# A hybrid encoder layer on one core: the convolution's layer norm goes from the first stage to the last, taps cover 1,024 tokens, and the projections get a fourth PSUM buffer

## The chip, the cores and the metric

The kernel runs on one core of one Trainium2 chip, as one launch. The metric is the device time of one execution, in microseconds (us); lower is better. An execution takes a little longer than the span of the profile, which goes from the first to the last instruction. Engines are named as in the profile: PE (TensorE matmuls), PEld (its weight loads), DVE (VectorE), ACT (ScalarE), POOL (GpSimd) and SP (SyncE, which here issues nearly all DMAs, in order, from one queue).

## What is computed

One encoder layer with the same weights for two groups of tokens, 2,048 and 1,024 of them, all float32. From `h = x @ w_in + b_in` (1,024 features in, 5,632 out, split in nine) two branches follow: a depthwise convolution of 31 taps with a layer norm and gates, and a differential attention with four heads. They are merged by sigmoid gates, projected, added to the input and normalised. The lines that matter here:

```python
u = glu_a * jax.nn.sigmoid(glu_b)
u = conv(u, conv_dw) + conv_dw_b            # 31 taps along the tokens, 512 channels
u = silu(layer_norm(u, conv_ln_g, conv_ln_b)) * silu(conv_gate)
y_conv = u @ w_conv_proj + b_conv_proj
...
merged = sigmoid(m_conv) * y_conv + sigmoid(m_attn) * (o @ w_attn_o)
out = layer_norm(ALPHA * x + merged @ w_out + b_out, ln_g, ln_b)
```

The layer norm of the convolution needs, for each token, the mean and the variance over all 512 channels. The channels lie on partitions, 128 to a tile, so these sums go over four channel tiles and over the partitions; the sum over partitions is a matmul with a matrix of constants (`ones_c`).

## The kernel before

**Precision.** Each float32 operand of a matmul is split into a rounded high part and the remainder (`split`, `split_w`: ACT copies, then DVE or POOL subtracts), and each product is three matmuls: high by high, low by high, high by low (`mm3`, `mm`).

**Phase A (0 to about 1549 us): the input projection.** Three blocks of 1,024 tokens, (group 0, first half), (group 0, second half), (group 1). In each, 22 weight pieces of 256 output features are worked through in the order of L211: GLU_B, GLU_A, GLU_B+1, GLU_A+1, K, CGATE, K+1, CGATE+1, Q, AGATE, and so on, then V and the merge gates. A piece has two output tiles, each 128 features by 1,024 tokens: 48 matmuls of 512 columns into one PSUM tile `psA` (L291). I count tiles from 0, so that tiles 2, 3, 6 and 7 are GLU_A, tiles 8 and 9 are K, 10 and 11 are CGATE, and so on. There are three `psA` buffers (L108), and two small ones, `psB`, for the layer norm. A tile is evacuated by `evac`: GLU_A by DVE (L238), K and Q by ACT and DVE (L254, L255; then the rotation by POOL at L259 and L260, and DVE at L262), gates by ACT and DVE (L242, L243), the merge gates by ACT alone (L248). POOL also makes the low part of every weight piece (`wl`, L127, two per piece).

The convolution runs in the same phase on DVE. GLU_A's product is written to DRAM (`ud`, L239); a generator, `conv_chunk`, handles 512 tokens of all four channel tiles. It loads `uc` (L150), does 31 taps for each channel tile (L156 the first, L159 the others; two channel tiles in turn), sums the tiles on POOL (L164 to L166), gets the mean by two matmuls (`total`, L139), subtracts it (L173), squares (L177), gets the variance in the same way, takes root and reciprocal (L186, L189), applies scale, gain, bias and SiLU (L193 to L198), and stores the result `sd` (L199). `pump` advances this generator by 6 or 11 steps after each output tile. The order of instructions on the engines in this phase and in phase C is set by a scheduler at build time; each engine then runs its list in order.

**Phase B (about 1549 to 2230 us): attention,** with an order written out by hand on PE, DVE, ACT and POOL: scores (L505), softmax, the combination of the two maps on POOL (L525 to L527, each with `e` of 128x1024), turns through the PE (L534, `tp`, copied out by ACT L536 and DVE L541), products (L95 to L97 into `ops`), and the sums of squares for the sub-layer norm (L566, L90 `sql`). At the end of it `prepare` (L419) makes the first input of phase C: it loads `sd` and the convolution's gate `cgd`, multiplies (L428) and splits the product into `uh` and `ul`.

**Phase C (about 2230 us to the end): merge and output.** Six rows of 512 tokens. For each row `merge` has eight steps of 24 matmuls (12 with `uh`, `ul` and 12 with `oh`, `ol`, into `y`, L95 to L97) and `project` has two halves of 96 matmuls (into `z`). The inputs of the next row are prepared during the projection of this one: `u` in its first half, `o` in its second. DVE also finishes each row (L705 to L722), and POOL makes the low part of each piece of `w_out` (`zl`).

Of the kernel before, what the change touches and what calls it, by code (L numbers as in the profile page):

```python
# [43 lines left out]
def encoder_kernel(ctx: ExitStack, tc: tile.TileContext, t: dict):  # L44
# [54 lines left out]
    # ---------------------------------------------------------------- phase A  # L99
    with ExitStack() as st:  # L100
# [34 lines left out]
        def total(x):  # L135
            """The mean over the channels, on every partition, of what the partitions hold of it."""
            ps = psB.tile([P, 512], F32, name="psB")
            for i, part in enumerate(split(cv, "tt", x, [P, 512], 1, nc.gpsimd)):
                nc.tensor.matmul(ps, ones_c, part, start=i == 0, stop=i == 1)  # L139
            return ps  # L140

        def conv_chunk(g, n):
            """The depthwise convolution of 512 tokens, its layer norm and SiLU, a step at a time."""
            t0 = n * 512
            acc = cv.tile([P, CT, 512], F32, name="acc")
            for c0 in range(0, CT, 2):
                us = []
                for c in (c0, c0 + 1):
                    u = cv.tile([P, 512 + 2 * HALO], F32, name="uc", bufs=3)
                    nc.sync.dma_start(u, ud[g][c][:, t0:t0 + 512 + 2 * HALO])  # L150
                    us.append(u)
                for k in range(TAPS):
                    for c in (c0, c0 + 1):
                        src = us[c - c0][:, k:k + 512]
                        if k == 0:
                            nc.vector.tensor_scalar(acc[:, c], src, dw_sb[:, c, 0:1], cvec[:, 0, c:c + 1],  # L156
                                                    op0=ALU.mult, op1=ALU.add)
                        else:
                            nc.vector.scalar_tensor_tensor(acc[:, c], src, dw_sb[:, c, k:k + 1], acc[:, c],  # L159
                                                           op0=ALU.mult, op1=ALU.add)  # L160
                        yield
            tmp = lambda: cv.tile([P, 512], F32, name="cvtmp", bufs=4)
            sm, sm2 = tmp(), tmp()
            nc.gpsimd.tensor_add(sm, acc[:, 0], acc[:, 1])  # L164
            nc.gpsimd.tensor_add(sm2, acc[:, 2], acc[:, 3])
            nc.gpsimd.tensor_add(sm, sm, sm2)  # L166
            for _ in range(4):
                yield
            mean = total(sm)
            for _ in range(3):  # L170
                yield
            for c in range(CT):
                nc.vector.tensor_sub(acc[:, c], acc[:, c], mean)  # L173
                yield
            for c in range(CT):
                s = cv.tile([P, 512], F32, name="cvsq", bufs=2)
                nc.scalar.activation(s, acc[:, c], AF.Square)  # L177
                if c:
                    nc.gpsimd.tensor_add(s, q2, s)
                q2 = s  # L180
                yield
            for _ in range(4):
                yield
            var = total(q2)
            sd_, rs = tmp(), tmp()
            nc.scalar.activation(sd_, var, AF.Sqrt, bias=eps_t)  # L186
            for _ in range(3):
                yield
            nc.vector.reciprocal(rs, sd_)  # L189
            for _ in range(5):  # L190
                yield
# [644 lines left out]
```

## Time and profile before

| | |
|---|---|
| time, median of 3 runs | 2825.17 us (2818.87 to 2825.88) |
| span of the profiled execution | 2816.1 us |
| PE busy | 2709.3 us (96%), 13,818 matmuls |
| DVE, ACT, POOL busy | 1843.1, 1074.4, 1478.5 us |
| phase A, 0 to 1549 us | PE 1478.49, DVE 862.90, POOL 653.03 us busy |
| 1549 to 2230 us (attention) | PE 671.07, DVE 595.87, POOL 603.76 us busy |
| 2300 to 2816 us (most of phase C) | PE 495.84, DVE 339.88, POOL 192.32 us busy |

The median of the runs lies 9.1 us above the span of the profiled execution, whose own time is close to that: what lies around the span is start and end of the execution. How to read the rows further down: a row of a timeline gives the start in us, the duration of the group in us, the engine, the line of the kernel, the operation, what it writes and reads by the program's names, the size, and in square brackets how long the engine sat idle before it and what it then waited for. A group's duration goes to the recorded end of its last instruction; the start of the next row on the same engine shows how long it really took from the queue. A row of the waits gives engine, tile and line, what ended the wait, the total in us, how often, and the longest.

### The profile page before, as it was taken

How to read it: one execution, taken by the hardware profiler on the slowest of the kernel's cores; microseconds unless marked ns; L12 is line 12 of the kernel's file. 1: busy time of each engine (PE TensorE's matmuls, PEld its weight loads, DVE VectorE, ACT ScalarE, POOL GpSimd, SP SyncE). 2: the span in 40 equal slices, each digit the busy share in tenths (PEclk: the TensorE clock that was granted, in tenths of full speed). 3: DMA queues.
4: the chain of work that ended last, by engine and by line, in shares of the span. 5: the costliest groups of instructions: out<-in, count | busy, mean ns of one | idle time of the engine just before them, and what ended most of it. 6: DMA issues, size and time to landing. Idle time of an engine off the chain costs nothing. (4 is left out here: it accounts for less than half of the span.)

```text
span 2816.1 us, 36981 instructions
## 1 busy us (share of the span) xinstructions
PE 2709.3 (96%) x13818; PEld 2274.5 (81%) x13818; DVE 1843.1 (65%) x2564; ACT 1074.4 (38%) x1540; POOL 1478.5 (53%) x774
## 2 busy tenths in 40 slices
PE   9989999998999998979999999999999999999998
PEld 7868988887897877858878788888888877777777
DVE  4961110396387495994940888888888866667665
ACT  3122132212322222213121788878788822222121
POOL 3554232245535424546442899988888833333343
PEclk9999999999999999989999999999999999999999
DMA  6245323324443343334333332322234375566553
GB/s 194 71 152 179 126 105 112 143 72 158 157 142 119 108 138 104 105 127 156 105 116 112 109 85 88 85 69 70 69 94 116 104 253 190 182 207 200 181 162 119
DMA packets 194980, 364.89 MB, mean 130 GB/s; under 512 B 25088, under 2 KB 98288, under 8 KB 194800
## 3 DMA queue, kind: packets, MB, share of 16 engines
q1 hardware_dynamic: 193792, 362.22, 40.1%
q8 instruction: 109, 1.79, 0.3%
q14 instruction: 71, 0.58, 0.1%
q10 hardware_dynamic: 1008, 0.29, 0.1%
HBM read 242.67 MB, written 107.18 MB: 124 GB/s over the span
## 5 line engine op out<-in xcount | busy, mean ns | idle before, releaser
L127 POOL TENSOR_TENSOR wl<-raw,wh 128x1024 fp32r<-128x1024 f32 (+1 forms) x138 | 416.5, 3038 | 485.6 <-ACT wh L126 471.8
L291 PE MATMUL psA<-xh,wh 128*128 128x512 f32 x1920 | 600.6, 395 | 37.7 <-DVE ev L255 16.5
L159 DVE SCALAR_TENSOR_TENSOR acc<-uc,conv_dw,acc 128x512 f32<-128x512 f32 x720 | 608.5, 896 | 5.8
L291 PE MATMUL psA<-xl,wh 128*128 128x512 f32 x1920 | 598.6, 393 | 0.9 <-DVE xl L284 0.9
L291 PE MATMUL psA<-xh,wl 128*128 128x512 f32 x1920 | 597.7, 393 | 0.3 <-POOL wl L127 0.3
L291 PEld LDWEIGHTS psA<-xh,wh 128*128 128x128 f32 x1920 | 365.4, 191 | 116.9 <-DVE ev L255 17.8
L291 PEld LDWEIGHTS psA<-xl,wh 128*128 128x128 f32 x1920 | 365.4, 190 | 78.8 <-DVE xl L284 1.6
L291 PEld LDWEIGHTS psA<-xh,wl 128*128 128x128 f32 x1920 | 364.6, 190 | 77.6 <-POOL wl L127 1.0
L527 POOL TENSOR_TENSOR e<-e 128x2048 f32<-128x2048 f32 (+1 forms) x96 | 373.1, 3887 | 8.0
L505 PE MATMUL s<-km,qq 128*128 128x512 f32 x1280 | 352.3, 397 | 4.8 <-DVE e L507 4.4
L518 ACT ACTIVATE e<-e,mx 128x2048 f32<-128x2048 f32 (+1 forms) x192 | 329.5, 1716 | 1.2 <-DVE e L507 1.1
L507 DVE TENSOR_SCALAR_CACHE_REDUCE e<-s 128x1024 f32<-128x1024 f32 x192 | 233.4, 1216 | 77.1 <-PE s L505 75.7
L541 DVE TENSOR_TENSOR al<-tp,ah 128x512 fp32r<-128x512 f32 x320 | 220.1, 688 | 56.1 <-ACT ah L536 56.1
L505 PEld LDWEIGHTS s<-km,qq 128*128 128x128 f32 x1280 | 219.7, 189 | 41.3 <-DVE e L507 10.7
L126 ACT ACTIVATE wh<-raw 128x1024 fp32r<-128x1024 f32 (+1 forms) x138 | 134.0, 1012 | 285.0 <-PE psA L291 164.9
L536 ACT ACTIVATE ah<-tp 128x512 fp32r<-128x512 f32 x320 | 189.5, 593 | 98.7 <-PE tp L534 96.1
L90 POOL TENSOR_TENSOR zl<-zraw,zh 128x512 fp32r<-128x512 f32 x88 | 123.8, 1409 | 162.4 <-ACT zh L89 142.5
L95 PE MATMUL ops<-ah,vv 128*128 128x256 f32 x640 | 207.3, 324 | 0.2 <-ACT row L567 0.2
L534 PEld LDWEIGHTS tp<-ident,e 128*128 128x128 f32 x1280 | 158.6, 141 | 48.6 <-DVE al L541 3.7
L534 PE MATMUL tp<-ident,e 128*128 128x128 f32 x1280 | 193.3, 274 | 4.5 <-POOL e L527 3.0
L97 PE MATMUL ops<-al,vv 128*128 128x256 f32 x640 | 180.7, 282 | 0.7 <-DVE al L541 0.7
L96 PE MATMUL ops<-ah,vv 128*128 128x256 f32 x640 | 179.7, 281 | 0.0
(165 smaller groups left out, 4259.5 us busy)
## 6 DMA issues: line engine op xcount, KB each, us to landing
raw<-in_w_in SPq DMA_DIRECT2D x130, 512.0 KB
qq<-qd SPq DMA_DIRECT2D x384, 64.0 KB
zraw<-in_w_out SPq DMA_DIRECT2D x88, 256.0 KB
ev<-ev SPq DMA_DIRECT2D x96, 128.0 KB
kd<-ev SPq DMA_DIRECT2D x24, 512.0 KB
qd<-ev SPq DMA_DIRECT2D x24, 512.0 KB
vd<-ev SPq DMA_DIRECT2D x24, 512.0 KB
mcd<-evm SPq DMA_DIRECT2D x24, 512.0 KB
```

Source lines behind the costliest of these rows:

```text
L95: nc.tensor.matmul(ps, ah, bh, start=first, stop=False)
L97: nc.tensor.matmul(ps, ah, bl, start=False, stop=last)
L127: nc.gpsimd.tensor_sub(lo, raw, hi.bitcast(F32))
L159: nc.vector.scalar_tensor_tensor(acc[:, c], src, dw_sb[:, c, k:k + 1], acc[:, c], op0=ALU.mult, op1=ALU.add)
L291: nc.tensor.matmul(ps[:, n * 512:(n + 1) * 512], w[a][:, k, j * P:(j + 1) * P], B.xs[k][x][:, n * 512:(n + 1) * 512], start=k == 0 and a = ...
L505: nc.tensor.matmul(s[:, n * 512:(n + 1) * 512], p.qt[2 * c + i][:, j * P:(j + 1) * P], p.km[c, hf][:, n * 512:(n + 1) * 512], start=i == 0 ...
L507: nc.vector.tensor_scalar(p.e[j, c][:, hf * 1024:(hf + 1) * 1024], s, -SCALE, mx[:, hf - 1:hf] if hf else None, op0=ALU.mult, op1=ALU.min, ...
L518: nc.scalar.activation(e, e, AF.Exp, bias=p.mx[j, c][:, nh - 1:nh], scale=-1.0, accum_out=sc)
L527: nc.gpsimd.tensor_add(e0, e0, e)
L534: nc.tensor.transpose(tp[:, i, j * P:(j + 1) * P], p.e[j, 0][:, kt * P:(kt + 1) * P], ident)
L536: nc.scalar.activation(ah, tp, AF.Copy)
L541: nc.vector.tensor_sub(al, tp, ah.bitcast(F32))
```

## The change

**The convolution.** `conv_chunk` becomes `conv_unit`: one channel tile and about 1,024 tokens (1,008, 1,040 and 1,024 in the three blocks, so that each block's taps need only what is there). A unit has one load of `uc`, 31 taps of that width (after: L144, L146) and one store of the plain convolution to `sd` (L148). Four units per block, 372 taps in all where there were 744 of 512 tokens. `uc` and `acc` have two buffers each. `pump` advances by 4 steps after each tile in every block.

**The layer norm** and SiLU leave phase A and stand in `prepare_u`, a generator with eight steps: load four tiles of `sd`; sum them on POOL (`sum4`, L403 to L405, the split at L407 and L408); two matmuls for the mean (L414); subtract and square (L424, L426), sum again; two matmuls for the variance; root and reciprocal (L432, L433) and the loads of `cgd`; and twice two tiles of scale (L443), sigmoid (L444), gain and bias (L445), gate times sigmoid on POOL (L446), product (L447) and split. For the first row these steps stand at the end of phase B, with PSUM taken from the turns' buffers `tp`; for the other five they stand in the projection of the row before, with PSUM taken from `y`. The `o` branch is unchanged, under the name `prepare_o`.

**PSUM.** With `psB` gone, `psA` has four buffers in place of three.

Comments are dropped, and one build setting (`dynamic_dma_scratch_size=1024`) is added.

```diff
-        psA = pool(name="a_ps", bufs=3, space=PSUM)
-        psB = pool(name="a_ps2", bufs=2, space=PSUM)
+        psA = pool(name="a_ps", bufs=4, space=PSUM)
...
-            rate = 6 if bi == 0 else 11
+            rate = 4
...
-                todo = [0, 1] if B.g else ([0] if B.b == 0 else [1, 2, 3])
-                convs += [conv_chunk(B.g, n) for n in todo]
+                t0, t1 = {(0, 0): (0, TB - 16), (0, 1): (TB - 16, 2 * TB), (1, 0): (0, TB)}[B.g, B.b]
+                convs += [conv_unit(B.g, i, t0, t1) for i in range(CT)]
...
+        def conv_unit(g, c, t0, t1):
+            n = t1 - t0
+            u = cv.tile([P, CONV_N + 2 * HALO], F32, name="uc", bufs=2)[:, :n + 2 * HALO]
+            nc.sync.dma_start(u, ud[g][c][:, t0:t1 + 2 * HALO])
+            acc = cv.tile([P, CONV_N], F32, name="acc", bufs=2)[:, :n]
+            for k in range(TAPS):
+                src = u[:, k:k + n]
+                if k == 0:
+                    nc.vector.tensor_scalar(acc, src, dw_sb[:, c, 0:1], cvec[:, 0, c:c + 1], op0=ALU.mult, op1=ALU.add)
+                else:
+                    nc.vector.scalar_tensor_tensor(acc, src, dw_sb[:, c, k:k + 1], acc, op0=ALU.mult, op1=ALU.add)
                 yield
+            nc.sync.dma_start(sd[g][c][:, t0:t1], acc)
...
+    def prepare_u(R, ps):
+        g, r = R.g, slice(R.t0, R.t0 + 512)
+        xs = []
+        for i in range(CT):
+            xs.append(cin.tile([P, 512], F32, name="lx", bufs=CT))
+            nc.sync.dma_start(xs[i], sd[g][i][:, r])
+        tmp = lambda tag: cin.tile([P, 512], F32, name="l" + tag, tag=tag, bufs=2)
+        def sum4(parts):
+            a, b = tmp("x1"), tmp("x2")
+            nc.gpsimd.tensor_add(a, parts[0], parts[1])
+            nc.gpsimd.tensor_add(b, parts[2], parts[3])
+            nc.gpsimd.tensor_add(a, a, b)
+            hi, lo = (cin.tile([P, 512], F32R, name="lm" + x, tag="rb", bufs=2) for x in "hl")
+            nc.scalar.activation(hi, a, AF.Copy)
+            nc.gpsimd.tensor_sub(lo, a, hi.bitcast(F32))
+            return hi, lo
+        def mean(parts):
+            m = ps()
+            for i, part in enumerate(parts):
+                nc.tensor.matmul(m, ones_c, part, start=i == 0, stop=i == 1)
+            return m
+        yield
+        parts = sum4(xs)
+        yield
+        m = mean(parts)
+        yield
+        sq = []
+        for x in xs:
+            nc.vector.tensor_sub(x, x, m)
+            sq.append(cin.tile([P, 512], F32, name="lq", bufs=CT))
+            nc.scalar.activation(sq[-1], x, AF.Square)
+        parts = sum4(sq)
+        yield
+        m = mean(parts)
+        yield
+        rs = tmp("x1")
+        nc.scalar.activation(rs, m, AF.Sqrt, bias=eps_t)
+        nc.vector.reciprocal(rs, rs)
+        gates = []
+        for i in range(CT):
+            gates.append(cin.tile([P, 512], F32, name="lq", bufs=CT))
+            nc.sync.dma_start(gates[i], cgd[g][i][:, r])
+        yield
+        for h in range(2):
+            for i in (2 * h, 2 * h + 1):
+                x = xs[i]
+                sg = tmp("x2")
+                nc.vector.tensor_mul(x, x, rs)
+                nc.scalar.activation(sg, x, AF.Sigmoid, bias=cvec[:, 2, i:i + 1], scale=cvec[:, 1, i:i + 1])
+                nc.vector.tensor_scalar(x, x, cvec[:, 1, i:i + 1], cvec[:, 2, i:i + 1], op0=ALU.mult, op1=ALU.add)
+                nc.gpsimd.tensor_mul(gates[i], gates[i], sg)
+                nc.vector.tensor_mul(x, x, gates[i])
+                R.ins["u"].append(split(cin, "u", x, [P, 512], 4))
+            yield
...
-                    ahead = prepare(rows[0], "u")
-                    for i in range(CT + 2):
+                    ahead = prepare(rows[0], "u", lambda: psT.tile([P, 512], F32, name="tp"))
+                    for i in range(U_STEPS):
                         late[now + 2 * i].append(lambda: next(ahead))
```

The change moves instructions at many places. Three of them are shown, each engine's own list, in order.

**DVE in the first block of phase A,** from the evacuation of tile 8 on. Before (L255 and L243 are evacuations, L159 taps, L262 the low part of the rotated K):

```order
L255 SCALAR_TENSOR_TENSOR ev<-psA,b_in_cols,cos 128x1024
L159 SCALAR_TENSOR_TENSOR acc<-uc,conv_dw,acc 128x512 x13
L262 TENSOR_TENSOR ev<-ev 128x1024
L159 SCALAR_TENSOR_TENSOR acc<-uc,conv_dw,acc 128x512 x3
L255 SCALAR_TENSOR_TENSOR ev<-psA,b_in_cols,cos 128x1024
L159 SCALAR_TENSOR_TENSOR acc<-uc,conv_dw,acc 128x512 x10
L243 SCALAR_TENSOR_TENSOR ev<-psA,b_in_cols,ev 128x1024
L159 SCALAR_TENSOR_TENSOR acc<-uc,conv_dw,acc 128x512 x2
L262 TENSOR_TENSOR ev<-ev 128x1024
L159 SCALAR_TENSOR_TENSOR acc<-uc,conv_dw,acc 128x512 x11
L243 SCALAR_TENSOR_TENSOR ev<-psA,b_in_cols,ev 128x1024
```

Now (L203 and L191 are the evacuations, L144 and L146 taps, L210 the low part):

```order
L203 SCALAR_TENSOR_TENSOR ev<-psA,b_in_cols,cos 128x1024
L146 SCALAR_TENSOR_TENSOR acc<-uc,conv_dw,acc 128x1008 x7
L210 TENSOR_TENSOR ev<-ev 128x1024
L146 SCALAR_TENSOR_TENSOR acc<-uc,conv_dw,acc 128x1008
L203 SCALAR_TENSOR_TENSOR ev<-psA,b_in_cols,cos 128x1024
L146 SCALAR_TENSOR_TENSOR acc<-uc,conv_dw,acc 128x1008
L144 TENSOR_SCALAR acc<-uc,conv_dw,conv_vecs 128x1008
L146 SCALAR_TENSOR_TENSOR acc<-uc,conv_dw,acc 128x1008 x5
L191 SCALAR_TENSOR_TENSOR ev<-psA,b_in_cols,ev 128x1024
```

Between two evacuations stand about as many tap elements as before, in half as many instructions. In the first block the taps of before end at tile 12; now they go on until tile 19, and 78 of them stand between the evacuation of tile 8 and that of tile 19. In the list of after the second and the third block look much the same as the first.

**POOL at the end of attention.** Before, the last two combinations of a pair (`cc`, `e`, `e`) stand behind each other:

```order
L90 TENSOR_TENSOR sql<-sq,sqh 128x256
L525 TENSOR_TENSOR cc<-cc,stats 128x1
L526 TENSOR_SCALAR e<-e,cc,neglam 128x1024
L527 TENSOR_TENSOR e<-e 128x1024
L525 TENSOR_TENSOR cc<-cc,stats 128x1
L526 TENSOR_SCALAR e<-e,cc,neglam 128x1024
```

Now the sums over the channel tiles stand between them, and those of the squares (`lq`) right behind:

```order
L91 TENSOR_TENSOR sql<-sq,sqh 128x256
L534 TENSOR_TENSOR cc<-cc,stats 128x1
L535 TENSOR_SCALAR e<-e,cc,neglam 128x1024
L536 TENSOR_TENSOR e<-e 128x1024
L403 TENSOR_TENSOR lx_18556<-lx 128x512
L404 TENSOR_TENSOR lx_18557<-lx 128x512
L405 TENSOR_TENSOR lx_18556<-lx_18556,lx_18557 128x512
L408 TENSOR_TENSOR lml<-lx_18556,lmh 128x512
L534 TENSOR_TENSOR cc<-cc,stats 128x1
L535 TENSOR_SCALAR e<-e,cc,neglam 128x1024
L536 TENSOR_TENSOR e<-e 128x1024
L91 TENSOR_TENSOR sql<-sq,sqh 128x256
```

So four instructions on POOL came in ahead of the last combination. On PE the two mean matmuls (L414) stand ahead of the last seven turns, and the two variance matmuls ahead of the last three.

**DVE at the same place.** Before, a product and a low part (L428, L90) stand between the copies of turned blocks (L541):

```order
L541 TENSOR_TENSOR al<-tp,ah 128x512 x2
L428 TENSOR_TENSOR x_19266<-x_19266,x_19267 128x512
L90 TENSOR_TENSOR ul<-x_19266,uh 128x512
L541 TENSOR_TENSOR al<-tp,ah 128x512 x2
L428 TENSOR_TENSOR x_19306<-x_19306,x_19307 128x512
L90 TENSOR_TENSOR ul<-x_19306,uh 128x512
```

Now (L424 subtracts the mean, L433 is the reciprocal, `lx_18747` the inverse root):

```order
L424 TENSOR_TENSOR lx<-lx,tp 128x512 x4
L550 TENSOR_TENSOR al<-tp,ah 128x512 x4
L433 RECIPROCAL lx_18747<-lx_18747 128x512
L550 TENSOR_TENSOR al<-tp,ah 128x512
L443 TENSOR_TENSOR lx<-lx,lx_18747 128x512
L445 TENSOR_SCALAR lx<-lx,conv_vecs 128x512
L447 TENSOR_TENSOR lx<-lx,lq 128x512
L91 TENSOR_TENSOR ul<-lx,uh 128x512
L443 TENSOR_TENSOR lx<-lx,lx_18747 128x512
L445 TENSOR_SCALAR lx<-lx,conv_vecs 128x512
L447 TENSOR_TENSOR lx<-lx,lq 128x512
```

The four channel tiles stand one behind the other: the scaling of the second tile (L443) follows the low part of the first (L91). In the rows of phase C that come later the four L443 stand together.

More of the change, by code (lines that the diff above doesn't have):

```diff
@@ L36 @@
 NE = 8
+CONV_N = TB + 16
 NST = NH * sum(LENS) // P
@@ L133, in load_w @@
             return w
[L135 to L167, printed above, removed]
-                yield
[L169 to L191, printed above, removed]
-            for c in range(CT):
-                nc.vector.tensor_mul(acc[:, c], acc[:, c], rs)
-                sg = cv.tile([P, 512], F32, name="cvsq", bufs=2)
-                nc.scalar.activation(sg, acc[:, c], AF.Sigmoid, bias=cvec[:, 2, c:c + 1], scale=cvec[:, 1, c:c + 1])
-                nc.vector.tensor_scalar(acc[:, c], acc[:, c], cvec[:, 1, c:c + 1], cvec[:, 2, c:c + 1],
-                                        op0=ALU.mult, op1=ALU.add)
-                nc.gpsimd.tensor_mul(acc[:, c], acc[:, c], sg)
-                nc.sync.dma_start(sd[g][c][:, t0:t0 + 512], acc[:, c])
-                yield
@@ L417, in __init__, with prepare, prepare_o @@
             self.ins, self.gates, self.m, self.x, self.st = {"u": [], "o": []}, [], [], [], []
-    def prepare(R, kind):
+    def prepare(R, kind, ps=None):
+        return prepare_u(R, ps) if kind == "u" else prepare_o(R)
+    def prepare_o(R):
         g, r = R.g, slice(R.t0, R.t0 + 512)
-        dst = R.ins[kind]
+        dst = R.ins["o"]
         loaded = []
@@ L425, in prepare @@
             if i >= 2:
[L426 to L432 removed]
+                x1, x2, rb = loaded.pop(0)
+                nc.vector.scalar_tensor_tensor(x1, x1, gsub, x2, op0=ALU.mult, op1=ALU.mult)
@@ L433, in prepare @@
+                nc.vector.tensor_mul(x1, x1, rb)
+                dst.append(split(mp, "o", x1, [P, 512], 4))
             if i < CT:
-                src = [d[g][i][:, r] for d in {"u": (sd, cgd), "o": (ogd, agd)}[kind]]
-                if kind == "o":
-                    src.append(rrd[g][i, r].partition_broadcast(P))
-                loaded.append([cin.tile([P, 512], F32, name=n, bufs=2) for n in ("x1", "x2", "rb")[:len(src)]])
+                src = [ogd[g][i][:, r], agd[g][i][:, r], rrd[g][i, r].partition_broadcast(P)]
@@ L438, in prepare @@
+                loaded.append([cin.tile([P, 512], F32, name=n, bufs=2) for n in ("x1", "x2", "rb")])
                 for x, y in zip(loaded[-1], src):
                     nc.sync.dma_start(x, y)
+            yield
+    U_STEPS = 8
+    def prepare_u(R, ps):
[51 more added lines that the diff above has]
+                R.ins["u"].append(split(cin, "u", x, [P, 512], 4))
@@ L775, in encoder_kernel @@
                 factors(1, io, psY.tile([P, 512], F32, name="y"))
-            steps = {kind: [lambda i=i: next(i)] * (CT + 2) if nxt else [] for kind in "uo"
-                     for i in [nxt and prepare(nxt, kind)]}
+            steps = {kind: [lambda i=i: next(i)] * n if nxt else [] for kind, n in (("u", U_STEPS), ("o", CT + 2))
+                     for i in [nxt and prepare(nxt, kind, lambda: psY.tile([P, 512], F32, name="y"))]}
             both = lambda *fs: lambda: [f() for f in fs]
```

9 lines of the change are left out of this document (1 added, 8 removed).

## The prediction

> **What bounds the kernel now.** I read the page first, then busy time by stretch, then PE's waits, then timelines where PE waits. The page and the windows:
>
> ```profile
> PE 2709.3 (96%) x13818; PEld 2274.5 (81%) x13818; DVE 1843.1 (65%) x2564; ACT 1074.4 (38%) x1540; POOL 1478.5 (53%) x774
> 0.00:1549.00 1549.00, 1478.49 (x6940) 1239.35 (x6940) 862.90 (x1011) 370.66 (x390) 653.03 (x262) 0.98 0.38 127
> 2230.00:2300.00 70.00, 63.87 (x316) 50.49 (x315) 44.41 (x56) 23.93 (x50) 29.41 (x23) 0.98 0.78 248
> 2300.00:2816.00 516.00, 495.84 (x2112) 394.78 (x2110) 339.88 (x446) 115.80 (x199) 192.32 (x133) 1.00 0.56 178
> ```
>
> The columns are the window, its length, then PE, PEld, DVE, ACT, POOL busy, the granted clock, DMA share, GB/s. PE bounds every stage: only gaps, slow clock and the edges can be won. DVE is busy 863 of 1549 us in phase A, so on average it is no limit there; the question is whether it is one in places. PE's waits:
>
> ```profile
> PE psB L139 <- ACT tth L89: 28.5, 4, 13.6
> PE psA L291 <- DVE ev L255: 16.5, 3, 6.8
> PE psA L291 <- DVE ev L243: 11.9, 4, 5.0
> PE psA L291 <- ACT xh L283: 5.4, 1, 5.4
> PE psA L291 <- ACT evm L248: 3.9, 1, 3.9
> PE psB L139 <- POOL ttl L90: 3.2, 3, 2.1
> ```
>
> Of 69 us here, 32 are the layer norm's matmuls (`psB`), which stand in PE's list ahead of projections that could run, and 32 are evacuations that come late (28 of them DVE's, behind taps). How much phase A loses in all comes from the pace of undisturbed matmuls:
>
> ```profile
> 1240.30 0.62 PE L291 MATMUL psA<-xh,wh 128*128 128x512 f32 x2
> ...
> 1256.17 0.61 PE L291 MATMUL psA<-xh,wl 128*128 128x512 f32 x2
> ```
>
> There are 35 pairs between these starts: 15.87/70 = 0.227 us a matmul, 10.88 us for a tile of 48. The 6940 of the window are 5760 such, 1152 of half the width (about 0.12) and the norm's 24: 1306 + 138 + 5 = 1449 us. So phase A loses 100 us: 69 in the waits above and the rest at a slow clock, as behind the longest wait:
>
> ```profile
> 1270.38 0.80 PE L139 MATMUL psB<-tth,ones_c 128*128 128x512 f32 x1 [13.61 <-ACT tth L89]
> ...
> 1273.85 1.05 PE L291 MATMUL psA<-xh,wh 128*128 128x512 f32 x2
> 1277.26 0.81 PE L291 MATMUL psA<-xl,wh 128*128 128x512 f32 x2
> ```
>
> The four pairs from 1273.85 to 1277.26 take 3.41 us where they take 1.81 at full pace, so a wait of this length costs about 1.6 us more. [...]
>
> **Part 1: the taps.** The first block, where K and the gates are evacuated:
>
> ```profile
> 126.34 1.28 DVE L255 SCALAR_TENSOR_TENSOR ev<-psA,b_in_cols,cos 128x1024 f32<-128x1024 f32 x1
> 127.53 16.09 DVE L159 SCALAR_TENSOR_TENSOR acc<-uc,conv_dw,acc 128x512 f32<-128x512 f32 x13
> 143.55 1.21 DVE L262 TENSOR_TENSOR ev<-ev 128x1024 f32<-128x1024 f32 x1
> 144.69 2.06 DVE L159 SCALAR_TENSOR_TENSOR acc<-uc,conv_dw,acc 128x512 f32<-128x512 f32 x3
> ...
> 147.87 6.69 DVE L159 SCALAR_TENSOR_TENSOR acc<-uc,conv_dw,acc 128x512 f32<-128x512 f32 x10
> 154.50 1.27 DVE L243 SCALAR_TENSOR_TENSOR ev<-psA,b_in_cols,ev 128x1024 f32<-128x1024 f32 x1
> ```
>
> ```profile
> 125.90 2.79 POOL L259 TENSOR_TENSOR ev<-ev,sin 128x1024 f32<-128x1024 f32 x1 [6.97 <-DMA ev<-ev]
> 128.78 2.72 POOL L260 TENSOR_TENSOR ev<-ev 128x1024 f32<-128x1024 f32 x1
> 133.62 5.48 POOL L127 TENSOR_TENSOR wl<-raw,wh 128x1024 fp32r<-128x1024 f32 x2 [2.12 <-ACT wh L126]
> ```
>
> Ten taps with POOL idle take 154.50 - 147.87 = 6.63 us, 0.663 each. Thirteen with POOL at work take 16.02: 7.4 us longer, while POOL ran 9.4 us (the last 1.2 of L259, L260 and the two L127). So 1 us of POOL costs the taps 0.79 us, and one POOL operation of 2.72 us costs DVE 2.15. The evacuation at 126.34 took 1.19 us to the next start beside POOL, so evacuations are not held up.
>
> [...]
>
> A tap of 1,024 tokens is not in the trace. Two of 512 take 1.33; the subtraction at 143.55, as wide and with two SBUF inputs, takes 1.14 to the next start. I take 1.20, nearer to the latter since one instruction's fixed part is saved. Over 372 taps that spares 372 x 0.13 = 48 us of DVE.
>
> Where DVE does not hold PE up, that is worth nothing. Where it does is counted from the order of after, with the first starts of GLU_A's evacuation and of the taps (each row: duration in ns as least, median, most; first and last start):
>
> ```profile
> L238 DVE SCALAR_TENSOR_TENSOR ev<-psA,b_in_cols,ev x12: 1271/1278/1285, 43.5 to 1112.7; 128x1024 f32<-128x1024 f32 x12
> L156 DVE TENSOR_SCALAR acc<-uc,conv_dw,conv_vecs x24: 534/547/2625, 54.5 to 1417.9; 128x512 f32<-128x512 f32 x24
> ```
>
> Tile 2 is ready at 43.5, so PE's first tile began about 10 us into the span (43.5 - 3 x 10.88), and tile 8 is ready at 10 + 9 x 10.88 = 108. In each block 46 taps stand ahead of its evacuation. From 54 us on, 46 x 1.20 + 3 x 1.19 + 7 POOL operations x 2.15 = 74, so it is evacuated at 128, much as now (126.34): DVE is 20 us behind. From there to the evacuation of tile 19 there are 78 taps, 11 evacuations of 1.19, six subtractions of 1.14 and 24 POOL operations (12 for the rotation, 12 for weights), of which one in twelve falls beside an evacuation: 93.6 + 13.1 + 6.8 + 22 x 2.15 = 161 us. PE's 11 tiles are 120. So DVE falls behind by 41 more, 61 in all. Four `psA` buffers let PE run three tiles ahead, 32.6 us (three: 21.8). The rest, 28 us, is a wait on `psA` in each block, 85 in three, and at four waits a block 1.3 us of clock each, 15. With 10 at the start, phase A would lose 110, where it now loses 100 and 5 in the norm's matmuls: **+5 us**. The gain of the removed norm (32 us of waits and 5 of matmuls) and of the fourth buffer (10.9 a block) is real, but the taps that stand spread over the second block's tiles now stand in front of tiles 8 to 19 of every block.
>
> Bounds: if a POOL operation costs DVE only 1.1 us, the wait is 28 - 23 = 5 a block, and A gains 64, some 69 with the clock; if taps cost 1.33 and POOL all of 2.72, it is 28 + 10 + 13 = 51, and A loses 75 to 80.
>
> **Part 2: the layer norm of row 0,** at the end of attention. Sizes, from the same operations in phase A of before:
>
> ```profile
> L173 DVE TENSOR_TENSOR acc<-acc,psB x24: 678/681/687, 365.0 to 1449.7; 128x512 f32<-128x512 f32 x24
> L189 DVE RECIPROCAL cvtmp<-cvtmp x6: 3352/3353/3354, 402.3 to 1474.7; 128x512 f32<-128x512 f32 x6
> L196 DVE TENSOR_SCALAR acc<-acc,conv_vecs x24: 536/598/2190, 408.1 to 1486.2; 128x512 f32<-128x512 f32 x24
> L195 ACT ACTIVATE cvsq<-acc,conv_vecs x24: 799/816/820, 406.4 to 1485.3; 128x512 f32<-128x512 f32 x24
> L195 ACT ACT_TABLE_LOAD  x6: 1283/1283/1283, 402.3 to 1474.7; - x6
> L198 POOL TENSOR_TENSOR acc<-acc,cvsq x24: 1285/1300/2297, 408.7 to 1490.4; 128x512 f32<-128x512 f32 x24
> L165 POOL TENSOR_TENSOR cvtmp<-acc x6: 1260/1265/1291, 179.7 to 1442.4; 128x512 f32<-128x512 f32 x6
> ```
>
> And where PE, ACT and POOL stand there now (from their timelines):
>
> ```profile
> 2234.13 0.60 PE L534 MATMUL tp<-ident,e 128*128 128x128 f32 x4
> 2236.56 0.63 ACT L89 ACTIVATE uh<-x 128x512 fp32r<-128x512 f32 x1 [2.04 <-DVE x L428]
> 2235.93 0.65 POOL L525 TENSOR_TENSOR cc<-cc,stats 128x1 f32<-128x1 f32 x1
> 2240.62 1.17 POOL L90 TENSOR_TENSOR sql<-sq,sqh 128x256 fp32r<-128x256 f32 x1
> 2256.96 0.54 PE L97 MATMUL y<-ul,w_conv_projh 128*128 128x512 f32 x1
> ```
>
> POOL is free for the sums at 2235.93, where the last combination stands now. Three sums, ACT's copy, the low part: 4 x 1.27 + 0.63 = 5.7, so the mean can run at 2241.6, where PE arrives at about 2234: 7.5 us of wait. The last combination (4.7) ends at 2246.4, `sql` at 2247. The subtractions (4 x 0.68, behind four copies of turns) and squares are done by about 2248; the second sums end at 2254. PE has meanwhile done the turns up to there and waits about 5 us. From the variance: root with table load 2.0, reciprocal 3.35, first tile at 2259.5. A tile then goes through DVE 0.68, ACT 0.82, POOL 1.30, DVE 0.68, ACT 0.63, DVE 0.69 = 4.8 us, and the next starts only then: with one more table load (1.28), the four are ready at about 2265.5, 2270.5, 2275 and 2280. PE then lacks nothing of the first output tile of `u`, a state that before is reached with the row at 2256.96. **+23 us**; nothing else is queued on PE for that time, since `y` of the second output tile needs the same inputs. If sums and squares slip less and a tile takes 3.5 us, 12; if POOL is held by DVE at each step, 32.
>
> **Part 3: rows 1 to 5 of phase C.** In the order of after, mean and variance stand behind 36 and 96 of the 192 projecting matmuls, and the next row's first `y` behind 164. Four more matmuls per row are 0.9 us. The chain from variance to the first `uh`, 2.0 + 3.35 + 0.68 + 1.28 + 0.82 + 1.30 + 0.68 + 0.63 = 10.7, has 68 x 0.227 = 15.4 us; but the fourth tile is due at about 24 and DVE has, from the reciprocal on, 3.35 + 4 x (0.68 + 0.6 + 0.68 + 0.69) = 14 us for `u` beside POOL's work, which is held to 0.79 of some 10 us more: just in time. I take 1.5 us of wait a row: 5 x 2.4 = **+12 us**, bounds 0 and 35.
>
> The remaining edits (build setting, comments) cost nothing that a row could show. Sum: 5 + 23 + 12 = +40 on the span of 2816.1; the 9.1 us from span to median stay: 2856 + 9 = **2865 us**.
>
> **The rivals.**
> 1. *DVE keeps up* (faster). Against it: the 7.4 us above, and 28 us of waits on DVE's evacuations now. For it: 48 us spared, a fourth buffer, and wider taps that might meet POOL less often. [...] At 1.1 us a POOL operation A gains 69; with 18 and 4 for parts 2 and 3: 2816 - 47 + 9 = 2778. It decides from about 1.6 us a POOL operation down, where the sum is no change.
> 2. *It cancels*: at that price, 2825.
> 3. *Phase C becomes DVE's* (slower still): 340 of 516 us busy there now; a row adds 4 x (0.68 + 0.68 + 0.60) + 3.35 = 11 us of DVE and 8 x 1.27 + 4 x 1.30 = 15 of POOL. At 10 us a row: 5 + 23 + 50, so 2903.
> 4. *Phase A slower by the upper bound*: +80 + 35 gives 2940.
>
> **How the numbers follow.** About 0.3% (8.5 us) is what can be told from no change. Chances: forecast 0.50, DVE keeps up 0.25, cancels 0.13, C bound 0.08, upper bound of A 0.04. Faster 0.25, same 0.13, slower 0.62. The range from 2785 to 2905 leaves out most of rival 4 and the better half of rival 1; given slower it is 2835 to 2905.
>
> **What would show it.** Right: `psA` waits on DVE's evacuations at tiles 12 to 23 of each block, 20 to 35 us a block; DVE without a pause there; no `psB`; taps of about 1.20; POOL operations each costing taps about 2 us; PE idle for 20 us in 2235 to 2285, on the mean and `uh`. Wrong: phase A shorter than 1500 us, or `u` ready before the turns end.

## The result, and the profile after

The changed kernel takes 2928.74 us (median of 4 runs, 2926.51 to 2934.08) where the kernel before, timed beside it, takes 2823.98: a ratio of 1.0382, 95% interval 1.0366 to 1.0397. Slower was forecast, but by 40 us and with an upper end of 2905; it is 105.

The span is 2926.6 us in place of 2816.1, 110.5 more. That is 6 us more than the medians differ by: the profiled execution of the kernel before was a quick one, its span lies 2.8 us under the shortest of its times (2818.87), and in each run of the changed kernel the time is 1.8 us above the span. The page's first line, and busy time of phase A and of the five later rows of phase C (each row of `y` and `z` counted from the end of the last `y` of the row before):

```profile
PE 2752.8 (94%) x13818; PEld 2300.0 (79%) x13818; DVE 1855.0 (63%) x2192; ACT 1069.7 (37%) x1540; POOL 1443.3 (49%) x774
0.00:1555.00 1555.00, 1482.00 (x6911) 1238.51 (x6912) 781.76 (x561) 309.31 (x311) 526.58 (x190) 0.98 0.39 127
2345.20:2876.90 531.70, 483.92 (x1957) 381.28 (x1956) 393.71 (x473) 154.21 (x249) 249.84 (x178) 0.95 0.52 166
```

The same five rows before, of which the prediction had no view of its own:

```profile
2306.40:2766.00 459.60, 447.08 (x1904) 355.88 (x1902) 310.95 (x404) 105.87 (x181) 175.46 (x120) 1.00 0.59 189
```

So the 110.5 us come in three parts. The first scores of attention start at 1555.3 in place of 1548.0: phase A +7.3. The last `y` of row 0 ends at 2345.2 in place of 2306.4, 38.8 later: the end of attention and row 0 +31.5. The five later rows take 531.7 in place of 459.6: +72.1, 14.4 a row, and the granted clock there is 0.95 in place of 1.00. After that nothing more is lost (49.7 us to the end, 50.1 before). PE's waits:

```profile
PE y L96 <- ACT uh L90: 27.3, 9, 6.5
PE psA L239 <- ACT wh L126: 23.6, 6, 8.0
PE psA L239 <- DVE ev L191: 19.7, 9, 3.8
PE y L96 <- DVE ma L700: 16.2, 4, 4.5
PE y L96 <- DVE mc L699: 15.4, 12, 2.2
PE psA L96 <- ACT wh L126: 11.4, 3, 6.5
PE tp L414 <- DVE al L550: 9.8, 2, 5.9
PE y L98 <- DVE ul L91: 8.0, 6, 1.5
...
PE psA L98 <- POOL wl L127: 5.8, 3, 2.0
PE psA L239 <- POOL wl L127: 5.5, 7, 1.3
```

Waits on `psA` are phase A, `tp` and some of `uh` the end of attention, and `ma`, `mc` (the products with the merge gates) are new (0.2 us before): PE waits in the merge for DVE.

**Phase A, where the lag shows up.** As forecast, DVE hardly pauses while a block's taps run (2.7 us from 125 to 289), but PE's longest waits are on weights. One of them, followed back over five engines, each from its own timeline:

```profile
174.31 1.27 DVE L191 SCALAR_TENSOR_TENSOR ev<-psA,b_in_cols,ev 128x1024 f32<-128x1024 f32 x1
```

```profile
174.41 0.32 SPq L148 DMA_DIRECT2D sd<-acc  x1
...
175.61 0.43 SPq L193 DMA_DIRECT2D cgd<-ev  x1
176.13 0.43 SPq L114 DMA_DIRECT2D raw<-in_w_in  x1
176.66 3.08 SPq L206 DMA_DIRECT2D ev<-ev  x4
```

```profile
187.01 2.47 POOL L207 TENSOR_TENSOR ev<-ev,sin 128x1024 f32<-128x1024 f32 x1 [19.61 <-DMA ev<-ev]
189.56 3.18 POOL L208 TENSOR_TENSOR ev<-ev 128x1024 f32<-128x1024 f32 x1
194.86 5.66 POOL L127 TENSOR_TENSOR wl<-raw,wh 128x1024 fp32r<-128x1024 f32 x2 [2.11 <-ACT wh L126]
```

```profile
192.78 1.06 ACT L209 ACTIVATE ev<-ev 128x1024 fp32r<-128x1024 f32 x1 [28.23 <-POOL ev L208]
193.74 1.99 ACT L126 ACTIVATE wh<-raw 128x1024 fp32r<-128x1024 f32 x2
```

```profile
194.83 1.22 PE L239 MATMUL psA<-xh,wh 128*128 128x512 f32 x2 [8.03 <-ACT wh L126]
```

The gate's evacuation at 174.31, late behind taps, ends at 175.5. In SP's queue the rotation's copies (L206) stand behind the store of a convolution tile (L148), which goes out when its taps are done, and behind the gate's store (L193). ACT's half of K's evacuation had ended at 164.55; the copies are issued at 176.66. POOL waits 19.61 us for them, ACT waits 28.23 for POOL, and the weights for PE stand behind that in ACT's list. A late evacuation so reaches PE by the queues of three other engines before the PSUM buffers run out. All nine waits on `wh` look like this one: ACT has just come from a wait of 26.5 to 29.9 us for POOL, and POOL from one of 16.0 to 20.7 us for copies that were issued behind a gate's store.

**The end of attention.** PE's timeline:

```profile
2247.88 0.79 PE L414 MATMUL tp<-lmh,ones_c 128*128 128x512 f32 x1 [5.91 <-DVE al L550]
2261.31 0.79 PE L414 MATMUL tp<-lmh,ones_c 128*128 128x512 f32 x1 [3.90 <-DVE al L550]
...
2278.14 0.79 PE L96 MATMUL y<-uh,w_conv_projh 128*128 128x512 f32 x1 [4.17 <-ACT uh L90]
2283.68 0.79 PE L96 MATMUL y<-uh,w_conv_projh 128*128 128x512 f32 x1 [3.73 <-ACT uh L90]
2292.27 0.80 PE L96 MATMUL y<-uh,w_conv_projh 128*128 128x512 f32 x1 [6.52 <-ACT uh L90]
2297.59 0.80 PE L96 MATMUL y<-uh,w_conv_projh 128*128 128x512 f32 x1 [3.67 <-ACT uh L90]
```

Mean, variance and then the four channel tiles one by one, as worked out; with phase A's 7.3 us taken off, the mean at 2240.6 (forecast 2241.6), the variance at 2254 (2254), the tiles at 2270.8 to 2290.3 (2265.5 to 2280). The waits named for the two `tp` rows are put down to DVE, whose copy `al` ended just before (at 2247.82 the first time) and freed a `tp` buffer. What held it was POOL: ACT's copy of the sum (`lmh`, 2245.98) had waited 5.89 us for the sums, the copy `ah` (2246.52) stood behind it in ACT's list, and `al` (2247.13) needs `ah`.

**A row of phase C.** DVE in the row from 2454 to 2563, and its busy time in the stretch:

```profile
2473.41 1.28 DVE L730 TENSOR_TENSOR xr<-xr,z 128x512 f32<-128x512 f32 x2 [9.88 <-PE z L98]
...
2477.59 3.33 DVE L433 RECIPROCAL lx<-lx 128x512 f32<-128x512 f32 x1
...
2500.95 0.68 DVE L91 TENSOR_TENSOR ul<-lx,uh 128x512 fp32r<-128x512 f32 x1
...
2523.93 2.75 DVE L720 SCALAR_TENSOR_TENSOR xr<-xr,mv,ln_g_b 128x1024 f32<-128x1024 f32 x2
2526.61 0.68 DVE L91 TENSOR_TENSOR ol<-x,oh 128x512 fp32r<-128x512 f32 x1
...
2527.34 4.85 DVE L725 SCALAR_TENSOR_TENSOR xr<-xr,mv,ln_b_b 128x1024 f32<-128x1024 f32 x4
2532.11 1.88 DVE L700 TENSOR_TENSOR ma<-y,ma 128x512 f32<-128x512 f32 x3
```

```profile
2475.00:2497.00 22.00, 18.89 (x77) 14.68 (x77) 21.86 (x20) 9.38 (x14) 14.52 (x10) 0.93 0.43 126
2497.00:2520.00 23.00, 21.70 (x85) 16.86 (x84) 20.62 (x30) 8.17 (x15) 8.42 (x6) 0.92 0.57 177
2520.00:2542.00 22.00, 16.28 (x52) 12.29 (x51) 19.79 (x23) 2.52 (x4) 7.82 (x5) 0.77 0.58 203
```

```profile
2532.85 0.80 PE L96 MATMUL y<-oh,w_attn_oh 128*128 128x512 f32 x1 [3.55 <-DVE ma L700]
```

DVE is busy 62 of these 67 us (third of the busy columns), PE 57. The finishing of the row before (L720, L725) stands ahead of `ma`, three `ma` are done in a bunch at 2532, and PE has waited for the first. Before the change, the same part of a row looks like this:

```profile
2421.44 0.69 DVE L90 TENSOR_TENSOR ol<-x,oh 128x512 fp32r<-128x512 f32 x1 [0.70 <-ACT oh L89]
...
2445.18 1.28 DVE L721 TENSOR_TENSOR xr<-xr,z 128x512 f32<-128x512 f32 x2 [15.50 <-PE z L97]
```

```profile
2446.00:2468.00 22.00, 22.00 (x96) 17.75 (x95) 22.00 (x31) 3.72 (x8) 6.53 (x4) 1.00 0.52 156
```

DVE had the next row's `o` branch done (the last `ol` at 2421.44) ahead of the additions of the first half of `z`, and then waited 15.50 us for the second half. From there on it was full, 22.00 of 22 us, with the second additions, the finishing and the products, and PE at full pace beside it. Now the norm's operations, from the reciprocal at 2477.59 to the last `ul` at 2500.95, stand in the gap between the two halves of `z`, and the `o` branch has moved behind them (its last `ol` at 2526.61), into the stretch that was full.

### The profile page after: what moved, and what is told of

Its sections match the earlier page's. It is cut to its first block, busy times and chain, and to the rows that moved or that the text cites. A ratio compares the mean times of both kernels' runs of the same rounds, so it can differ in the third digit from the quotient of the medians.

```text
span 2926.6 us, 36610 instructions
## 1 busy us (share of the span) xinstructions
PE 2752.8 (94%) x13818; PEld 2300.0 (79%) x13818; DVE 1855.0 (63%) x2192; ACT 1069.7 (37%) x1540; POOL 1443.3 (49%) x774
## 3 DMA queue, kind: packets, MB, share of 16 engines
q10 hardware_dynamic: 1008, 0.29, 0.1%
## 4 chain that ended last, share of the span: by engine, by line
PE 58%; DVE 27%; issue 6%; DMA 5%; POOL 3%; ACT 1%; SPq 1%; DVEq 0%; POOLq 0%; ACTq 0%
PE psA L239 21%; DVE acc L146 17%; PE s L514 9%; PE tp L543 4%; PE ops L96 2%; PE ops L98 2%; PE ops L97 2%; PE y L96 2%; PE y L98 2%; PE y L97 2%; PE z L96 2%; PE z L97 2%; PE z L98 2%; PE psA L98 2%; PE psA L96 2%
## 5 line engine op out<-in xcount | busy, mean ns | idle before, releaser
L127 POOL TENSOR_TENSOR wl<-raw,wh 128x1024 fp32r<-128x1024 f32 (+1 forms) x138 | 382.5, 2790 | 677.1 <-ACT wh L126 677.1
L146 DVE SCALAR_TENSOR_TENSOR acc<-uc,conv_dw,acc 128x1008 f32<-128x1008 f32 (+2 forms) x360 | 598.1, 1714 | 1.7
L232 DVE TENSOR_TENSOR xl<-raw,xh 128x1024 fp32r<-128x1024 f32 (+1 forms) x25 | 32.6, 1306 | 325.7 <-ACT xh L231 325.7
L207 POOL TENSOR_TENSOR ev<-ev,sin 128x1024 f32<-128x1024 f32 x24 | 71.1, 2961 | 311.7 <-DMA ev<-ev 263.7
L96 PE MATMUL ops<-ah,vv 128*128 128x256 f32 x640 | 208.3, 325 | 0.2 <-ACT row L576 0.2
L91 POOL TENSOR_TENSOR zl<-zraw,zh 128x512 fp32r<-128x512 f32 x88 | 122.9, 1397 | 138.1 <-ACT zh L90 106.9
```

The source lines that it names most:

```text
L96: nc.tensor.matmul(ps, ah, bh, start=first, stop=False)
L127: nc.gpsimd.tensor_sub(lo, raw, hi.bitcast(F32))
L146: nc.vector.scalar_tensor_tensor(acc, src, dw_sb[:, c, k:k + 1], acc, op0=ALU.mult, op1=ALU.add)
```

## The experiments

All ratios are to the kernel before, timed beside the run on the same chip. A difference in us to the changed kernel or to another experiment is one of medians from different chips, on which the kernel before took 2818.6 to 2824.0; a few us between them say nothing.

**1. Without the norm.** The plain convolution is stored by phase A as now, and phase C multiplies it with the gate.

```diff
-        return prepare_u(R, ps) if kind == "u" ...     # norm, SiLU, product
+        # loads of sd and cgd, tensor_mul, split: as in the kernel before
```

> This kernel leaves the layer norm and the SiLU of the convolution out altogether; phase C multiplies the plain convolution with the gate, as before the change. Taps, fourth PSUM buffer and order of phase A stay as in the changed kernel. Theory (the loss is the norm's work in phase C and at the end of attention; phase A is about even): phase A within 5 us of 1555, phase C and the boundary as in the kernel before, in all 2824 + 7 = 2825 to 2838. Rival (the wide taps, the fourth buffer or the build setting cost the time, also in phase C): over 2870.

Measured: 2825.05 us, ratio 1.0015 (1.0006 to 1.0025). Phase A ends at 1554.4, and the five rows take 461.6 us (459.6 before). The 105 us shrink to 4: all but phase A's few us of the loss hangs on the norm's work at the end of attention and in phase C.

**2. One more reciprocal a row.**

```diff
         nc.vector.reciprocal(rs, rs)
+        if R is not rows[0]:
+            dummy = tmp("x2")
+            nc.vector.reciprocal(dummy, rs)
```

> The changed kernel with one more reciprocal of 128x512 per row on DVE (rows 1 to 5), right behind the norm's own; nothing reads its result. Theory (DVE is the bound from the middle of the projection to the middle of the merge): each adds its full 3.3 us or more, 5 x 3.3 to 5 x 5 = 16 to 25 us, 2945 to 2954. Rival (PE waits for a chain with idle time of DVE in it, which takes up the extra work later in the row): 0 to 8 us, below 2937.

Measured: 2950.36 us, ratio 1.0459 (1.0440 to 1.0478), 21.6 more than the changed kernel: 4.3 us for each 3.3. The extra work is not taken up anywhere. But DVE's list has it ahead of the scaling, so the chain to `u` grew as well, and the build put other instructions of DVE in a new order too: in the five rows PE now waits 24.7 us on `oh`, and on `ma` 7.9. So this run alone does not tell the two apart.

**3. Gain and bias on ACT.**

```diff
-                nc.vector.tensor_scalar(x, x, cvec[:, 1, i:i + 1], cvec[:, 2, i:i + 1], op0=ALU.mult, op1=ALU.add)
+                nc.scalar.activation(x, x, AF.Identity, bias=cvec[:, 2, i:i + 1], scale=cvec[:, 1, i:i + 1])
```

> The changed kernel with gain and bias of the norm (four tensor_scalar per row) on ACT in place of DVE. They are not on the chain to u, since sigmoid and the product with the gate take longer beside them. Theory (DVE's time bounds): each took 0.6 us alone and 1.5 us beside POOL, so 2.4 to 6 us a row, 12 to 36 us over six rows, 2893 to 2917. Rival (the chain's latency bounds): 0 to 5 us either way, 2924 to 2934.

Measured: 2918.21 us, ratio 1.0345 (1.0327 to 1.0363), 10.5 less: 1.75 a row. The direction is the theory's, the size is below its range. Here too the build changed DVE's order beyond the edit (in the five rows the waits on `uh` go from 9.2 to 0.7 us, and 8.9 on `oh` are new), so the 10.5 us are not the price of these four operations alone.

**4. Taps four per tile.** DVE's order in phase A by hand.

```diff
+        st.enter_context(tc.manual_schedule(engines={mybir.EngineType.DVE}))
         for si, (bi, c) in enumerate(seq):
...
+                    old = lows[:]        # low parts of K and Q, one tile later
+                    lows.clear()
                     evac(B, c, j, ps)
-                    pump(rate)
+                    pump(rate // 2)
+                    for f in old:
+                        f()
+                    pump(rate - rate // 2)
```

> The changed kernel with DVE's order in phase A as the program writes it: four taps behind each evacuation from the first K tile on, and K's and Q's low part one tile later. The same instructions, but 42 taps in place of 78 between tiles 8 and 19. Theory (DVE's lag there, and what hangs on it through the DMA queue, POOL and ACT, is what phase A loses): phase A ends 50 to 85 us earlier, at 1470 to 1505, in all 2845 to 2880. Rival A (the loss comes from POOL held up by DVE in any case): back-to-back taps in the tiles of the merge gates starve POOL and the weights come late: phase A not below 1540. Rival B (order does not matter, DVE and POOL share too much): within 10 us of 2929.

Measured: 2828.39 us, ratio 1.0025 (1.0015 to 1.0034), 100 us less than the changed kernel, more than expected. In the trace the lists of ACT and POOL are those of the changed kernel. Phase A, and all that PE waits for in it:

```profile
0.00:1454.00 1454.00, 1447.93 (x6913) 1221.73 (x6914) 823.67 (x561) 311.80 (x311) 497.19 (x190) 1.00 0.42 135
```

```profile
PE psA L242 <- ACT xh L234: 5.3, 1, 5.3
PE psA L242 <- DVE xl L235: 0.8, 1, 0.8
```

Only the start is left, at the full clock: 1454 is the 1444 us of matmuls worked out in the prediction and 10 at the start. So DVE's order (taps and low parts), with the same instructions, is worth all that phase A lost. The kernel before loses nearly as much there (105 us by the prediction), so the 100 us only make up for the rest of the change, which stays: behind phase A this run takes 1372 us, the changed kernel 1371. Rival A fell too: 44 taps in a row in the tiles of the merge gates (332.56 to 401.4 in the first block) did not make weights late.

**5. Three PSUM buffers, with the taps spread.**

```diff
-        psA = pool(name="a_ps", bufs=4, space=PSUM)
+        psA = pool(name="a_ps", bufs=3, space=PSUM)
```

> e4_spread (taps four per tile) with three psA buffers in place of four. In e4_spread PE never waits on psA, so the question is how much of that the fourth buffer gives. Theory (order of the taps is what counts): DVE's lag stays below the 21.8 us that three buffers allow nearly everywhere, 0 to 15 us more than e4_spread's 2828. Rival (the fourth buffer makes the gain): 10.9 us a block and more, 30 to 60 us, 2860 to 2890.

Measured: 2830.57 us, ratio 1.0033 (1.0021 to 1.0046), first scores at 1454.2. With taps in a good order the fourth buffer gives nothing that can be told: the intervals of the two runs overlap.

**6 and 9. Phase C's order by hand,** on DVE and PE, on top of experiment 4: norm steps in the merge and the first half of the projection (6); then with the additions of `z` ahead of the norm's last steps (9).

```diff
+        st.enter_context(tc.manual_schedule(engines={mybir.EngineType.DVE, mybir.EngineType.PE}))
...
-            first = steps["u"] + ...
+            first = [step, nothing, nothing, step, step, nothing, step, step]          # 6
+            first = [nothing, nothing, nothing, step, step, nothing, step, nothing]    # 9
```

> e4_spread with the orders of DVE and PE in phase C as the program writes them, and the steps of the next row's norm placed apart: loads, sums and mean in the merge, subtraction at the start of the projection, variance three steps later, the rest in its first half. The same work. Theory (the norm's DVE work is placed by the scheduler where DVE is already full, from the half of the projection on; DVE has room elsewhere in the row): 5 to 10 us a row less than e4_spread, 2778 to 2803. Rival (a row of phase C has no room for 11 us more of DVE and 15 of POOL, wherever they stand): within 10 us of 2828 or worse.

> e6_c_spread with the first half of z added ahead of the norm's last steps: variance at the fourth step of the projection, reciprocal at the fifth, two channel tiles at the seventh, the other two at the start of the second half, residual in the first four steps. In e6_c_spread PE waited 110 us for z's PSUM buffers, whose additions stood behind the norm in DVE's list. Theory (placing of DVE's work, not its amount, costs the time of phase C): 5 to 10 us a row less than e4_spread's 108, 2775 to 2805. Rival (a row has no room for it on DVE beside POOL): rows stay at 105 or more, 2820 or more.

Measured: 2915.35 us, ratio 1.0337 (1.0316 to 1.0358), and 2883.82, ratio 1.0226 (1.0207 to 1.0245): 87 and 55 us worse than experiment 4, where some 25 to 50 less was expected. In 6 PE waited 110 us for DVE's additions of `z`, which my order put behind the norm; in 9 it waited 27 us for them in four rows, 26 for the sums of the mean and 13 for `oh`. Neither order was good enough to say that none is. Whether a row of phase C has room for the norm stays open.

**7, 8 and 10. The norm back in phase A.** Taps spread by hand at five per tile (seven in the merge gates' tiles), then the norm by rows of 512 tokens reloaded from `sd`, its sums and its matmul held apart by whole tiles of PE's work; phase C as before the change. The three differ only in the tiles between loads and sums.

```diff
+        def norm(g, n):
+            ... load four tiles of sd
+            for _ in range(tiles):      # 7: 1    8: 3    10: 4 for a block's first row, 2 for others
+                yield "tile"
+            ... sums on POOL, split
+            yield "tile"
+            yield "tile"
+            m = total(p)                # mean, in a psA buffer
...
+                elif x == "tile":       # in pump: the rest waits for the next output tile
+                    break
```

> The plain taps of the changed kernel spread by hand over the tiles of phase A (five per tile, seven in the tiles of the merge gates), the layer norm and SiLU back in phase A, behind the taps of the same block, by rows of 512 tokens, with a tile or two of PE's work between the sums and the matmul that needs them; phase C and the end of attention as before the change. Theory (phase A has room for taps and norm when their order leaves evacuations in time, and phase C has none): phase A ends at 1460 to 1485, phases B and C as before, 2732 to 2765. Rival (DVE is too full in phase A for both): PE waits on psA again, 2780 or more.

> e7_norm_in_a with two more tiles of PE between the loads of a row and its sums on POOL. In e7_norm_in_a phase A ended at 1538 instead of about 1460, and 55 us of that were PE's mean matmuls waiting for sums that came late because the last unit's store and the reload were late. Theory: these waits go, phase A ends at 1460 to 1480, 2732 to 2755 in all. Rival (POOL, starved by taps, sets the time of the sums wherever they stand): the waits stay, 2790 or more.

> e8_norm_slack with four tiles between loads and sums for the first row of each block and two for the others (three for all in e8). In e8_norm_slack the first mean of each block still waited 4 to 7 us. Theory (these waits are only distance): they go, phase A ends 15 to 25 us earlier than 1497, 2740 to 2752 in all. Rival (the sums come late by POOL, which taps hold up, and the second row's matmuls wait instead): within 8 us of 2766.

Measured: 2809.13 us, ratio 0.9954 (0.9942 to 0.9966); 2765.94, ratio 0.9810 (0.9792 to 0.9829); 2748.49, ratio 0.9749 (0.9730 to 0.9768). Attention starts at 1538.0, 1497.4 and 1478.3. The first lies in its rival's range, but not by the rival's cause: PE's mean matmuls waited 55 us for their sums, as the norm's matmuls did in the kernel before, and nowhere for DVE's evacuations. The second had some of it left (16.9 us), and came out between its two ranges. The third came out as expected; its phase A, and PE's waits for the norm's sums:

```profile
0.00:1480.00 1480.00, 1461.33 (x6941) 1227.82 (x6942) 919.75 (x640) 369.55 (x391) 602.34 (x262) 1.00 0.44 142
```

```profile
PE psA L168 <- POOL nl L162: 4.2, 5, 0.9
PE psA L168 <- ACT nh L161: 4.1, 4, 2.4
```

It beats both kernels, by 71 us (2.5%) the kernel before. DVE does more in phase A (920 us) than in either, and PE hardly waits. What the kernel before would gain from its own taps spread by hand was not run.

**11 and 12. DVE work off the norm's chain left out** of the changed kernel: the residual's scaling and bias (11), or the two finishing multiplications (12).

```diff
-            nc.vector.scalar_tensor_tensor(R.x[tt], R.x[tt], ALPHA, bo, op0=ALU.mult, op1=ALU.add)    # 11
-            nc.vector.scalar_tensor_tensor(x, x, mv[:, 0:1], lg, op0=ALU.subtract, op1=ALU.mult)      # 12
-                nc.vector.scalar_tensor_tensor(x[:, c], x[:, c], mv[:, 3:4], lb[:, c], op0=ALU.mult, op1=ALU.add)    # 12
```

> The changed kernel without the scaling of the input and the bias of the output projection in phase C (four scalar_tensor_tensor of 128x1024 a row on DVE, 1.2 us each alone, which this kernel leaves out). They belong to the end of a row and are no part of the chain from the convolution to u. Theory (DVE's time bounds a row from the half of the projection to the middle of the merge): 4 to 6 us a row less, 24 to 36 us, 2893 to 2905. Rival (PE waits for the latency of the norm's chain): 0 to 8 us, 2921 or more.

> The changed kernel without the two multiplications with mean, gain, root and bias that finish a row's output (eight scalar_tensor_tensor of 128x1024 a row on DVE; left out here, but for the second of the last row). They are no part of the norm's chain either, but unlike the residual of e11_no_residual they stand in DVE's list ahead of the products with the gates (ma) for which PE waits in the merge; three of the residual's four move up in their place, so that five operations of 1.2 us less stand there. Theory (DVE's list from the half of the projection to those products is the bound): 4 to 7 us for each of rows 1 to 5, 20 to 35 us less, 2893 to 2908, and PE's waits on ma and mc go. Rival (what counts is the norm's chain up to u): the waits on ma and mc move to u, 0 to 8 us, 2920 or more.

Measured: 2925.38 us, ratio 1.0382 (1.0358 to 1.0406), the same ratio as the changed kernel's, which is the rival's; and 2894.63, ratio 1.0265 (1.0242 to 1.0287), 34 less, which is the theory's. The residual stands in DVE's list behind the `ma` for which PE waits; the finishing stands ahead of it. So it is not DVE's time in the row that counts, as the expectation for 11 had it, but what its list has in front of `ma`. PE's waits in the rows of 12:

```profile
PE y L96 <- ACT uh L90: 9.2, 5, 1.8
PE y L96 <- DVE mc L699: 7.0, 8, 1.6
...
PE y L96 <- DVE ma L700: 5.7, 4, 1.5
```

`ma` and `mc` fell from 31.6 to 12.7 us; the wait on `uh` stayed at 9.2 and that on `ul` at 6.4: this part belongs to the chain to `u`. Both causes are there, DVE's list the larger. The other instructions of DVE keep their order but for some 10 in 11 and 36 in 12.

## Why the prediction was right or wrong

*Phase A: right in the root, and in the sum partly by luck.* Forecast +5, measured +7.3; forecast 110 us lost, measured 1555 - 1444 = 111. The parts were off and made up for each other: behind the 10 us of the start, PE waits 67 us (forecast 85), and the other 34 (forecast 15) are slower matmuls. The 1.3 us of clock a wait in that 15 no run shows for a single wait; here 28 waits on evacuations and weights, 66 us, came with the 34, 1.2 each on average, where twelve were forecast. A tap took what was taken for it, and POOL cost the taps about what it had cost them, here in two places of the first block:

```profile
186.02 16.74 DVE L146 SCALAR_TENSOR_TENSOR acc<-uc,conv_dw,acc 128x1008 f32<-128x1008 f32 x7
202.68 1.21 DVE L210 TENSOR_TENSOR ev<-ev 128x1024 f32<-128x1024 f32 x1
...
225.32 8.33 DVE L146 SCALAR_TENSOR_TENSOR acc<-uc,conv_dw,acc 128x1008 f32<-128x1008 f32 x7
233.57 1.27 DVE L191 SCALAR_TENSOR_TENSOR ev<-psA,b_in_cols,ev 128x1024 f32<-128x1024 f32 x1
```

Seven taps with POOL idle take 8.25 us, 1.18 each (taken: 1.20). Seven beside 11.3 us of POOL (L207, L208 and two L127 above) take 16.66, 8.4 more: 0.74 for each us (taken: 0.79). Experiment 4 shows that the lag from DVE's order is the cause. Wrong was where it would be seen: 85 us on DVE's evacuations were forecast, 19.7 came there, and 46 on weights (`wh` 35.0, `wl` 11.3), by the DMA queue, POOL and ACT. I had followed only the PSUM buffers, not who else waits for a late evacuation.

*The gain of the fourth buffer,* 10.9 us a block, is at most a gain against a lag: experiment 5 has nothing of it when there is none, and with a lag it was not tested.

*The norm of row 0: right mechanism, term too small.* Forecast +23, within 12 to 32; measured +31.5. Mean and variance came within 1 us of the forecast; the tiles came 5.3 to 8.6 us apart in place of 5, and the first 5 us late. The price of a tile left out what else stands in the queues that it passes. The root, first of all, stood behind copies of turned blocks in ACT's list: the variance's matmuls start at 2261.31, the root's table load only at 2266.71. ACT at the third tile:

```profile
2287.46 0.63 ACT L90 ACTIVATE zh<-zraw 128x512 fp32r<-128x512 f32 x1 [3.56 <-DMA zraw<-in_w_out]
2288.00 0.80 ACT L444 ACTIVATE lx<-lx,conv_vecs 128x512 f32<-128x512 f32 x1
```

Its sigmoid stood behind the copy of a piece of `w_out`, which waited 3.56 us for its load.

*Phase C: the step that failed.* It said that DVE has "14 us for `u` beside POOL's work", due at 24, and so is "just in time": 1.5 us of wait and 0.9 of matmuls, 2.4 us a row. It measured 14.4 a row. The norm's own operations came out much as counted: 24 us from the reciprocal to the end of the last `ul`, and PE's waits on `uh` and `ul` are 15.7 us in five rows, 3.1 a row. What the sum left at nothing is what stands behind them in DVE's list: the `o` branch, the second additions of `z` and the finishing of the row, all of them ahead of `ma`. With the `o` branch moved there, a stretch that had been full already (22.00 of 22 us before the change) got longer, and PE waited 31.6 us for `ma` and `mc`. The trace of before showed that stretch; I read DVE's average over the phase (340 of 516). Rival 3 had the right mechanism but 10 us a row, and 0.08 of the chances.

Of the 72 us, 36 are more of PE's waits (47.9 in the five rows, 12.2 before). The rest is PE's busy time, 483.92 us in place of 447.08: 4.5 are the 20 added matmuls, and 32 are matmuls that run slower, a term that I had put into phase A and left at nothing here. The granted clock, 0.95 of the full one over 531.7 us, makes about 27 of the 32 (0.05 x 531.7, an estimate); the rest stays open. In the row from 2454, six waits of 0.55 to 3.55 us went with a granted clock of 0.93, 0.92 and, in the stretch with the two longest (2.17 and 3.55 us, 2520 to 2542), 0.77. That the waits bring the clock down is my reading of this; no run takes the two apart.

*The sum's last term,* 9.1 us from the span to the median, was not start and end of the execution: that is 1.8 us here. The rest was one quick execution against the median of three. It does not bear on the forecast of +40.

*DVE keeps up* (rival 1) fell for the order as it is; experiment 4 shows what it would have been worth (phase A of 1454 us in place of 1548). What the wide taps give in themselves was not measured: no run has taps of 512 tokens in that order.

## What to carry to other kernels

Before work is moved to another stage, look at the stretch of that stage where it will stand, and at what stands behind it in the same engine's list: an engine that is idle a third of the time on average, and idle just where the new work goes, can be full in the 22 us behind it. The build's scheduler had put the taps early, one behind the other; the same instructions, spread by hand so that each evacuation comes in time, took 100 us off. When an evacuation is late, follow all that waits for it, the DMA queue too, not only the buffers that it frees.

## What the runs showed of the hardware that I had not expected

DVE and POOL worked beside each other at a price of 0.79 us of DVE per us of POOL for taps of 512 tokens (13 taps, 7.4 us longer beside 9.4 us of POOL) and of 0.74 for taps of 1,008 (7 taps, 8.4 us longer beside 11.3); longer instructions made little difference. Of the 7 taps, the four that met an operation of POOL took 3.34 to 3.38 us, the others 1.26 at most. And the clock: in five rows of phase C, waits of 0.3 to 4.5 us, 36 us more of them than before, came with 32 us of slower matmuls, nearly as much again, while the 12.2 us of waits before the change left the clock of these rows at 1.00.
